# A hybrid encoder layer: softmax denominators moved behind the value products, key decay moved to ScalarE, sums of w_out moved into transfers

## The chip, the cores and the metric

The kernel runs on one core of a Trainium2 chip. TensorE (PE) multiplies, VectorE (DVE), ScalarE (ACT) and GpSimd (POOL) work element by element, SyncE (SP) issues transfers. Each engine works through its own instructions in order and waits for the others by semaphores. The metric is the device time of one execution in microseconds (us); the median of three runs of the kernel before is 1170.45 us (1169.81 to 1171.85).

## The reference, cut to what matters

One layer over 1024 tokens of width 1024: a combined input projection, two groups of mixer heads, an output projection, a layer norm, a SwiGLU with a second gated input, another layer norm. All arithmetic is float32. The change lies in the mixers:

```python
u = jnp.einsum('bsd,de->bse', h, w_in[i])
rq, rk, rv, rg, aq, ak, av = jnp.split(u, split_points, axis=-1)
y_ret = _bidirectional_retention(rq, rk, rv, lg_f, lg_b, ret_gn_gain[i], rg)   # 8 heads of 64
y_att = _windowed_gqa(aq, ak, av, attn_sink[i])                                # 8 q heads, 2 kv heads
mix = jnp.einsum('bse,ed->bsd', jnp.concatenate([y_ret, y_att], axis=-1), w_out[i])
...
# windowed attention: blocks of 128 queries, 384 keys around them, ALiBi slope per head, a sink logit per head
scores = jnp.where(valid, scores + alibi, NEG_INF)
m = jnp.maximum(jnp.max(scores, axis=-1, keepdims=True), sink_l)
e = jnp.exp(scores - m)
denom = jnp.sum(e, axis=-1, keepdims=True) + jnp.exp(sink_l - m)
probs = e / denom
out = jnp.einsum('bnhgqs,bnshd->bnqhgd', probs, vb)
...
# retention, chunks of 128: keys times a decay per row and head, for either direction
kv = jnp.einsum('bhnsd,bhnse->bhnde', k * k_decay[None, :, None, :, None], v)
```

## The kernel before, in words

A float32 product is made of three products of a high part and a low part (`mm3`); the high part is copied by ACT, the low part is subtracted by DVE (`split`). The mixer stage lies at about 50 to 342 us. Its main stream on PE is the rest of the input projection, 128 columns at a time (`mtile`), cut into steps of three matmuls of 128x512, called ticks below. Between these steps, in an order written out by hand (`run` with its lists), PE does the small products of the mixers: `F` in such a list stands for an equal share of the ticks, `sco`, `trn`, `val` for the attention's scores, transposes and value products of a query block, `K`, `kv`, `Q`, `Y`, `E`, `M` for parts of the retention. PE's order is fixed by this list; the orders of ACT, DVE, POOL and SP in this stage are a scheduler's. There are four pairs of heads: for pair 0 the attention and then the retention, for pairs 1 to 3 both woven together, 48 ticks each.

Attention: for each of 8 query blocks (4 to a half, two heads g each) `scores(n)` makes the products, DVE adds the bias, scales and takes the row maximum from PSUM (L550) and negates it (L552), ACT takes the exponential and its row sum (L554), with one more column that POOL copied from the sink logits (L545). Three ticks later DVE takes the reciprocal of the sum (L558) and ACT scales the probabilities by it (L560). `turn(n)` transposes them on PE (L572) and ACT brings them to SBUF (L574); `values(n)` multiplies (L584), and after the fourth block of a half ACT evicts the output (L587).

Retention: `keys(q)` transposes the keys (L408) and DVE multiplies them by the decays from PSUM (L411). `evict` squares the output twice on ACT (L488, L489) and copies it on DVE (L490); `norm` sums the squares on PE (L498), DVE scales the row (L500), and then a chain of small steps brings the normaliser to all partitions: SP spreads the row (L505, tile sn), POOL takes the power (L508), SP stores (L511) and fetches (L515, tile kv or rb), DVE multiplies y by it (L519).

Beside that, weights for later stages are prepared ("presplit"): SP loads a block, DVE sums pieces where the later product wants sums (L638 for w_out, L663 for the gate), `put` splits the piece on ACT and DVE (L602, L603) and SP stores it to DRAM at once (L604). For w_out's blocks 2 and 3 and the small ones all puts of a block share one buffer, so each waits for the store before it.

After the mixers the output projection starts (products at L802 to L804); its left operands are splits of the mixers' outputs y and of sums of them (L71, L72, L869, L871).

Of the kernel before, what the change touches and what calls it, by code (L numbers as in the profile page):

```python
# [12 lines left out]
ALU = mybir.AluOpType  # L13
# [17 lines left out]
LAG = 3  # L31
# [11 lines left out]
def layer(tc, xT, xn, w_first, w_mt, w_rv, w_out, w_pg, w_pe, pT, w_gu, w_dn,  # L43
# [175 lines left out]
    nlg = cp.tile([P, 16], F32, name="nlg")  # L219
    dve.tensor_tensor(nlg, rr[:, 0:16], t_[:, 0:16], ALU.mult)  # L220
# [10 lines left out]
    def slope(i, g):  # L231
        return 2.0 ** -(i + 4 * g + 1)
# [11 lines left out]
    def ev_aq(b, qs, h, i):  # L244
        sl = slice(h * HF, (h + 1) * HF)
        for g in range(2):
            sc_ = 0.125 / slope(i, g)
# [33 lines left out]
    later, side, ticks = [], [], [0]  # L281

    def take(k):
        for _ in range(min(k, len(queue))):
            queue.pop(0)()
            ticks[0] += 1
            for what in (later, side):
# [105 lines left out]
    class Retention:  # L393
# [8 lines left out]
        def keys(self, q):  # L402

            i = self.i
            tb = bank("t", (P, 4, P))
            for j in range(4):
                n = 4 * q + j
                pe.transpose(tb[:, j, :], self.rk[:, n * P:(n + 1) * P], ident)  # L408
            kdec = self.kdec[q] = bt([P, 2, 4, P], ("qq", "pt")[q])
            for d in range(2):  # L410
                dve.tensor_tensor(  # L411
                    kdec[:, d].rearrange("p n (h e) -> p n h e", h=2),
                    tb.rearrange("p n (h e) -> p n h e", h=2),
                    kd[:, d, 2 * i:2 * i + 2].unsqueeze(1).unsqueeze(3).to_broadcast([P, 4, 2, 64]),
                    ALU.mult)
# [69 lines left out]
        def evict(self, hh):  # L485
# [4 lines left out]
            dve.tensor_copy(self.half(hh), of)  # L490
# [35 lines left out]
    class Attention:  # L526


        def __init__(self, i, y):
            self.i, self.y, self.qs = i, y, pairs[i][2]  # L530
            self.st, self.sc, self.pt, self.o, self.ready = {}, {}, {}, {}, set()

        def scores(self, n):
# [9 lines left out]
            sc = self.sc[n] = [bt([P, NKT + 4], "sc", NSC) for _ in range(2)]  # L543
            for g in range(2):
                pool.tensor_copy(sc[g][:, nk:nk + 1], skb[:, 2 * i + g:2 * i + g + 1])  # L545
            for g in range(2):
# [4 lines left out]
                                         skb[:, 2 * i + g:2 * i + g + 1], ALU.add, ALU.max, st_[:, 0, j, g:g + 1])  # L551
            dve.tensor_scalar(st_[:, 1, j, :], st_[:, 0, j, :], -1.0, None, ALU.mult)  # L552
            for g in range(2):
                act.activation(sc[g][:, :nk + 1], sc[g][:, :nk + 1], AF.Exp, bias=st_[:, 1, j, g:g + 1],  # L554
                               accum_out=st_[:, 2, j, g:g + 1])

            def scaled():
                behind(dve.reciprocal(st_[:, 3, j, :], st_[:, 2, j, :]))  # L558
                for g in range(2):
                    behind(act.activation(sc[g][:, :nk], sc[g][:, :nk], AF.Copy, scale=st_[:, 3, j, g:g + 1]))  # L560
                self.ready.add(n)

            later.append((ticks[0] + LAG, scaled))

        def turn(self, n):
            assert n in self.ready
            lo, hi = span(n)
            self.pt[n] = []
            for g in range(2):
# [5 lines left out]
                self.pt[n].append(p_)  # L575

        def values(self, n):
# [8 lines left out]
            if j == 3:  # L586
                act.activation(self.half(hh), self.o[hh], AF.Copy)  # L587
# [6 lines left out]
    rnd = dr.tile([8, P, 8], F32, name="rnd")  # L594
    pgd = dr.tile([7, 4, P, 2, HF], F32, name="pgd")
# [5 lines left out]
    def put(x, o, dst):  # L601
        behind(act.activation(o[:, 0, :], x, AF.Copy))  # L602
        behind(dve.tensor_tensor(o[:, 1, :], x, o[:, 0, :].bitcast(F32), ALU.subtract))  # L603
        sp.dma_start(dst, o.bitcast(F32))  # L604
# [19 lines left out]
    def presplit_out(kt, ops, start, gap, raws=()):  # L624
# [10 lines left out]
        def step(p, k, k2, i):  # L635
            x = hold[k]
            if k2 is not None:
                behind(dve.tensor_tensor(x, x, hold[k2], ALU.add))  # L638
# [4 lines left out]
            [(ticks[0] + start + 5 + gap * i, lambda i=i, a=a: step(*a, i)) for i, a in enumerate(todo)]  # L643
# [95 lines left out]
    with tc.manual_schedule(engines={mybir.EngineType.PE}):  # L739
# [45 lines left out]
        run([*V, F, F, F], 16)  # L785

# [1108 lines left out]
def const_table():  # L1895
# [10 lines left out]
    c[:, C_BASE:C_BASE + NKT] = np.where(d <= P, -d, np.float32(-1e33))  # L1906
# [68 lines left out]
```

## Time and profile before

| what | value |
|---|---|
| median of three runs | 1170.45 us (1169.81 to 1171.85) |
| the profiled execution | span 1166.3 us; nothing beside the span is given for it, the median is 4.2 us above |
| PE busy | 1154.7 us, 99% of the span |
| DVE / ACT / POOL busy | 903.6 / 576.1 / 124.4 us |
| chain that ended last | PE 94%, DVE 3%, DMA 1%, ACT 1% |
| granted PE clock | 0.998 |

A line such as "L411 DVE TENSOR_TENSOR ... x8 | 5.5, 684 | 0.1" reads: line 411 of the kernel, the engine, the operation, how often, then busy time in us, mean duration of one in ns, and idle time of the engine just before. A row of the chain gives start, duration and what. Matmuls overlap, so the distance between their starts, and not the duration of one, is what a further one costs.

### The profile page before, as it was taken

The numbers are of one execution on the slowest core, as the hardware profiler recorded it, in microseconds if no ns is written. First come the engines' busy times: TensorE is split into PE (matmuls) and PEld (weight loads), VectorE is DVE, ScalarE is ACT, GpSimd is POOL, SyncE is SP. The second block draws the span as 40 slices with busy tenths as digits, with TensorE's granted clock in tenths as the row PEclk, the third lists the DMA queues.
The fourth block names the chain that finished last, engine by engine and source line by source line (L and its number), as shares of the span: only waits on it lengthen the run. The fifth ranks groups of instructions, "written<-read, shape, count | busy, mean of one in ns | idle before, by whom it ended". The sixth has DMA issues, their size and how long they took to land.

```text
span 1166.3 us, 17917 instructions
## 1 busy us (share of the span) xinstructions
PE 1154.7 (99%) x6330; PEld 971.3 (83%) x6330; DVE 903.6 (77%) x1746; ACT 576.1 (49%) x1169; POOL 124.4 (11%) x182
## 2 busy tenths in 40 slices
PE   9999999999999999999999999999999999999997
PEld 7888888888887888888888888888888888888885
DVE  5666697877859788948999988889888976864678
ACT  5566358676756265214445433444344445552462
POOL 2001021202010020000000000000000020234243
PEclk9999999999999999999999999999999999999999
DMA  6345676646356955665232232232223289989978
GB/s 253 103 150 205 254 236 215 209 154 218 132 192 231 359 181 197 250 218 197 100 116 92 101 120 103 85 137 99 100 72 136 94 253 350 351 220 225 254 157 234
DMA packets 84377, 214.39 MB, mean 184 GB/s; under 512 B 12224, under 2 KB 17472, under 8 KB 84288
## 3 DMA queue, kind: packets, MB, share of 16 engines
q1 hardware_dynamic: 75504, 195.94, 47.6%
q0 software_dynamic: 8784, 17.31, 8.4%
q8 instruction: 50, 0.82, 0.3%
q14 instruction: 39, 0.32, 0.1%
HBM read 141.32 MB, written 62.16 MB: 174 GB/s over the span
## 4 chain that ended last, share of the span: by engine, by line
PE 94%; DVE 3%; DMA 1%; ACT 1%; issue 1%; POOL 0%; SPq 0%; DVEq 0%; POOLq 0%; ACTq 0%
PE bmm L802 8%; PE bmm L803 8%; PE bmm L804 8%; PE bt L802 6%; PE bt L803 6%; PE bt L804 6%; PE bmm L77 5%; PE bmm L78 5%; PE bmm L79 5%; PE bs L804 4%; PE bs L803 4%; PE bs L802 4%; PE bo L804 4%; PE bo L803 4%; PE bo L802 4%; PE bt L572 2%
## 5 line engine op out<-in xcount | busy, mean ns | idle before, releaser
L77 PE MATMUL bmm<-H,w 128*128 128x512 f32 x240 | 97.0, 404 | 0.0
L78 PE MATMUL bmm<-H,w 128*128 128x512 f32 x240 | 94.1, 392 | 0.0
L79 PE MATMUL bmm<-H,w 128*128 128x512 f32 x240 | 93.9, 391 | 0.0
L1561 POOL DMA_DIRECT2D h0b<-in_w_dn x24 | 21.6, 902 | 538.4 <-DVE ev L1367 503.6
L1387 ACT ACTIVATE ev<-ev 128x512 f32<-128x512 f32 x42 | 26.5, 631 | 103.7 <-DVE ev L1416 90.5
L77 PEld LDWEIGHTS bmm<-H,w 128*128 128x128 f32 x240 | 45.1, 188 | 11.0 <-issue 1.4
L79 PEld LDWEIGHTS bmm<-H,w 128*128 128x128 f32 x240 | 45.0, 188 | 10.2
L78 PEld LDWEIGHTS bmm<-H,w 128*128 128x128 f32 x240 | 45.1, 188 | 8.3 <-DVE H L72 0.4
L554 ACT ACTIVATE sc<-sc,st 128x385 f32<-128x385 f32 (+1 forms) x64 | 37.3, 586 | 27.1 <-DVE st L552 27.0
L550 DVE CUSTOM_DVE_ANT_0 sc<-cst,bs,skb 128x384 f32<-128x384 f32 (+1 forms) x64 | 34.9, 575 | 7.7 <-PE bs L549 7.4
L1416 DVE TENSOR_TENSOR ev<-ev,bt 128x512 f32<-128x512 f32 x44 | 30.1, 684 | 12.6 <-PE bt L804 12.5
L1367 DVE TENSOR_TENSOR ev<-ev,bs 128x256 f32<-128x256 f32 x63 | 25.6, 418 | 15.5 <-PE bs L804 14.7
L545 POOL COPY sc<-skb 128x1 f32<-128x1 f32 x64 | 17.4, 280 | 189.2 <-PE bt L572 163.2
L1389 DVE TENSOR_TENSOR ev<-ev 128x512 f32<-128x512 f32 x42 | 29.0, 691 | 10.6 <-ACT ev L1387 9.1
L802 PE MATMUL bmm<-H,u 128*128 128x512 f32 x92 | 36.1, 392 | 0.0
L803 PE MATMUL bmm<-H,u 128*128 128x512 f32 x92 | 36.0, 392 | 0.0
L804 PE MATMUL bmm<-H,u 128*128 128x512 f32 x92 | 35.8, 389 | 0.0
L71 ACT ACTIVATE H<-ln 128x512 fp32r<-128x512 f32 (+1 forms) x34 | 23.0, 679 | 24.1 <-DVE ln L1051 7.2
L560 ACT ACTIVATE sc<-sc,st 128x384 f32<-128x384 f32 (+1 forms) x64 | 34.2, 583 | 0.9 <-DVE st L558 0.9
L72 DVE TENSOR_TENSOR w<-raw,w 128x512 fp32r<-128x512 f32 x34 | 23.1, 688 | 13.9 <-ACT w L71 13.9
L574 ACT ACTIVATE ptr<-bt 128x384 f32<-128x384 f32 (+1 forms) x64 | 26.6, 458 | 12.9 <-PE bt L572 12.7
L802 PE MATMUL bmm<-H,w 128*128 128x512 f32 x84 | 32.9, 392 | 0.0
(802 smaller groups left out, 3903.0 us busy)
## 6 DMA issues: line engine op xcount, KB each, us to landing
ad<-ev SPq DMA_DIRECT2D x33, 512.0 KB, 2.6
pgd<-pro SPq DMA_DIRECT2D x28, 512.0 KB, 2.9
raw<-in_w_gu SPq DMA_DIRECT2D x22, 512.0 KB, 3.7
ln<-in_w_gu SPq DMA_DIRECT2D x22, 512.0 KB, 3.8
raw<-ad SPq DMA_DIRECT2D x40, 256.0 KB, 5.8
ln<-ad SPq DMA_DIRECT2D x37, 256.0 KB, 6.3
H<-in_w_dn SPq DMA_DIRECT2D x33, 256.0 KB, 7.1
wod<-aq SPq DMA_DIRECT2D x15, 512.0 KB, 2.7
```

Source lines behind the costliest of these rows:

```text
L77: pe.matmul(o, lh, rh, start=start, stop=False)
L78: pe.matmul(o, lh, rl, start=False, stop=False)
L79: recent[0] = pe.matmul(o, ll, rh, start=False, stop=stop).ins.name
L550: dve.tensor_tensor_reduce(sc[g][:, :nk], cst[:, tc0:tc0 + nk], b[:, :nk], slope(i, g), skb[:, 2 * i + g:2 * i + g + 1], ALU.add, ALU.max, ...
L554: act.activation(sc[g][:, :nk + 1], sc[g][:, :nk + 1], AF.Exp, bias=st_[:, 1, j, g:g + 1], accum_out=st_[:, 2, j, g:g + 1])
L560: behind(act.activation(sc[g][:, :nk], sc[g][:, :nk], AF.Copy, scale=st_[:, 3, j, g:g + 1]))
L574: act.activation(p_[:, :hi - lo, :], tb[:, :hi - lo, :], AF.Copy)
L802: pe.matmul(o, lh, rh, start=start, stop=False, skip_group_check=True)
L803: pe.matmul(o, lh, rl, start=False, stop=False, skip_group_check=True)
L804: pe.matmul(o, ll, rh, start=False, stop=stop, skip_group_check=True)
L1389: dve.tensor_tensor(c[:, 1, :], c[:, 0, :], c[:, 1, :], ALU.mult)
L1416: dve.tensor_tensor(get(name), ev[left][:, m, :], right, ALU.add)
```

## The change

The exponentials go into the value products undivided; the division follows them. For that the scores are kept with the opposite sign: the scale of the attention's queries and the distance table change sign, the row maximum becomes a minimum that is itself the bias of the exponential (which takes scale -1), so the negation (L552) goes, and the sink column on POOL goes too. When the fourth block of a half has its scores, `sums` (two ticks later) adds exp(sink - m) for all four blocks and takes one reciprocal. `spread` follows block 2's or 6's transposes: PE turns the 128x8 reciprocals to 8x128, ACT copies them to SBUF, SP stores them to DRAM one tick later and, from the fifth tick on, fetches them twice, each spread over 64 partitions, into the place of the output in y. After the fourth value product DVE multiplies PSUM by y there, in place of ACT's copy.

The keys' decay is four ACT copies with a scale for each half in place of two DVE products; retention's copy of its output goes from DVE to ACT. The pieces of w_out are summed by transfers that POOL issues, reading w_out again and adding into the loaded tile; the order of the seven puts changes with it. `put` no longer issues its store at once: the store comes with the next put into the same buffer, or 2.5 ticks later.

PE gets eight rows more and keeps its order otherwise. The new row stands behind the transposes of block 2 of pair 3 (bt is the PSUM tile of the transposes, sc the exponentials, st the reciprocals):

```order
L586 MATMUL bt_3280<-cst,sc_3156 128x128 x3
L586 MATMUL bt_3286<-cst,sc_3157 128x128 x3
L566 MATMUL bt_3286<-cst,st_3016 8x128
L545 MATMUL bs_3298<-k_410,aq_2893 128x384
L546 MATMUL bs_3298<-kz_412,aq_2893 128x384
```

Before, the first two rows (then at L572) were followed by the scores at once.

DVE at the start of pair 2, before (kd are the keys' decays, w a weight split, aq the next queries):

```order
L500 TENSOR_SCALAR kv_2288<-bo_2201 2x512
L72 TENSOR_TENSOR w_2335<-raw_2333,w_2335 128x512
L519 SCALAR_TENSOR_TENSOR y_1604<-y_1604,gn,kv_2116 128x512
L411 TENSOR_TENSOR qq_2330<-bt_2325,kd 128x512
L251 SCALAR_TENSOR_TENSOR aq_2248<-bmm_2254,aq_2248 64x512
L411 TENSOR_TENSOR qq_2330<-bt_2325,kd 128x512
L72 TENSOR_TENSOR w_2338<-raw_2333,w_2338 128x512
L251 SCALAR_TENSOR_TENSOR aq_2249<-bmm_2254,aq_2249 64x512
L411 TENSOR_TENSOR pt_2360<-bt_2355,kd 128x512 x2
```

and after the change:

```order
L499 TENSOR_SCALAR kv_2239<-bo_2147 2x512
L72 TENSOR_TENSOR w_2290<-raw_2288,w_2290 128x512
L518 SCALAR_TENSOR_TENSOR y_1581<-y_1581,gn,kv_2067 128x512
L251 SCALAR_TENSOR_TENSOR aq_2193<-bmm_2200,aq_2193 64x512
L251 SCALAR_TENSOR_TENSOR aq_2194<-bmm_2200,aq_2194 64x512
L72 TENSOR_TENSOR w_2293<-raw_2288,w_2293 128x512
```

The four products with kd are gone from this place; the multiplication by the fetched row (L518, before L519) keeps its place.

SP at the end of pair 3, before (ped are stores of the last puts, sn and rnd and rb the last norm chain, w the first load of the next stage):

```order
L604 DMA ped<-aq_3046 128x1024
L505 DMA sn_3719<-kv_3717 64x1x8 x2
L511 DMA rnd<-sn_3719 128x8
L604 DMA ped<-aq_3046 128x1024
L515 DMA rb_3720<-rnd 64x512 x2
```

and after the change (adn holds the reciprocals):

```order
L623 DMA ped<-aq_2974 128x1024
L571 DMA adn<-rows_3600 8x128
L843 DMA w_3738<-wod 128x1024
L575 DMA y_2277<-adn 64x4x128
L623 DMA ped<-aq_2974 128x1024
L575 DMA y_2277<-adn 64x4x128
L504 DMA sn_3621<-kv_3619 64x1x8 x2
L510 DMA rnd<-sn_3621 128x8
L514 DMA rb_3622<-rnd 64x512 x2
```

The last store and the three transfers of the reciprocals now stand ahead of the norm chain's first transfer (sn).

The diff, without the constants' sign and the tile that goes:

```diff
@@ decay_k
             behind(act.activation(e[:, d, :], cst[:, C_BASE + P:C_BASE + 2 * P], AF.Exp,
-                                  scale=nlg[:, 8 * d + 2 * i + h:8 * d + 2 * i + h + 1]))
+                                  scale=lg[:, 8 * d + 2 * i + h:8 * d + 2 * i + h + 1]))
@@ Retention.keys
             for d in range(2):
-                dve.tensor_tensor(
-                    kdec[:, d].rearrange("p n (h e) -> p n h e", h=2),
-                    tb.rearrange("p n (h e) -> p n h e", h=2),
-                    kd[:, d, 2 * i:2 * i + 2].unsqueeze(1).unsqueeze(3).to_broadcast([P, 4, 2, 64]),
-                    ALU.mult)
+                for h in range(2):
+                    e = slice(64 * h, 64 * h + 64)
+                    act.activation(kdec[:, d, :, e], tb[:, :, e], AF.Copy, scale=kd[:, d, 2 * i + h:2 * i + h + 1])
@@ Retention.evict
-            dve.tensor_copy(self.half(hh), of)
+            act.activation(self.half(hh), of, AF.Copy)
@@ Attention.scores
-            for g in range(2):
-                pool.tensor_copy(sc[g][:, nk:nk + 1], skb[:, 2 * i + g:2 * i + g + 1])
...
                 dve.tensor_tensor_reduce(sc[g][:, :nk], cst[:, tc0:tc0 + nk], b[:, :nk], slope(i, g),
-                                         skb[:, 2 * i + g:2 * i + g + 1], ALU.add, ALU.max, st_[:, 0, j, g:g + 1])
-            dve.tensor_scalar(st_[:, 1, j, :], st_[:, 0, j, :], -1.0, None, ALU.mult)
+                                         nskb[:, 2 * i + g:2 * i + g + 1], ALU.add, ALU.min, st_[:, 0, j, g:g + 1])
             for g in range(2):
-                act.activation(sc[g][:, :nk + 1], sc[g][:, :nk + 1], AF.Exp, bias=st_[:, 1, j, g:g + 1],
+                act.activation(sc[g][:, :nk], sc[g][:, :nk], AF.Exp, bias=st_[:, 0, j, g:g + 1], scale=-1.0,
                                accum_out=st_[:, 2, j, g:g + 1])
-
-            def scaled():
-                behind(dve.reciprocal(st_[:, 3, j, :], st_[:, 2, j, :]))
+            if j < 3:
+                return
+
+            def sums():
                 for g in range(2):
-                    behind(act.activation(sc[g][:, :nk], sc[g][:, :nk], AF.Copy, scale=st_[:, 3, j, g:g + 1]))
-                self.ready.add(n)
+                    behind(act.activation(st_[:, 1, :, g], st_[:, 0, :, g], AF.Exp, bias=skb[:, 2 * i + g:2 * i + g + 1]))
+                behind(dve.tensor_tensor(st_[:, 2], st_[:, 2], st_[:, 1], ALU.add))
+                behind(dve.reciprocal(st_[:, 3], st_[:, 2]))
...
+        def spread(self, hh, b):
+
+            rows, home = bt([8, P], "rows", 1), adn[2 * self.i + hh]
+            pe.transpose(b, self.st[hh][:, 3].rearrange("p j g -> p (j g)"), ident)
+            act.activation(rows, b, AF.Copy)
+            r = self.y[:, hh * HF:(hh + 1) * HF]
+
+            def store():
+                sp.dma_start(home, rows)
+
+            def fetch():
+                for g in range(2):
+                    sp.dma_start(r[64 * g:64 * g + 64].rearrange("p (j q) -> p j q", j=4),
+                                 home.rearrange("(j g) q -> g j q", g=2)[g].partition_broadcast(64))
+
+            later.extend((ticks[0] + at, f) for at, f in zip(LAGA[1:], (store, fetch)))
@@ Attention.turn, Attention.values
+                if g and n % 4 == 2:
+                    self.spread(n // 4, tb[0:8, 3, :])
...
-                act.activation(self.half(hh), self.o[hh], AF.Copy)
+                dve.tensor_tensor(self.half(hh), self.o[hh], self.half(hh), ALU.mult)
@@ put
+        if id(o) in unsaved:
+            unsaved.pop(id(o))()
         behind(act.activation(o[:, 0, :], x, AF.Copy))
         behind(dve.tensor_tensor(o[:, 1, :], x, o[:, 0, :].bitcast(F32), ALU.subtract))
-        sp.dma_start(dst, o.bitcast(F32))
+        unsaved[id(o)] = save = lambda: sp.dma_start(dst, o.bitcast(F32))
...
+        saves.append((ticks[0] + 2.5, due))
@@ presplit_out
-        def step(p, k, k2, i):
-            x = hold[k]
-            if k2 is not None:
-                behind(dve.tensor_tensor(x, x, hold[k2], ALU.add))
-            put(x, ops[i % len(ops)], wod[p - 1, kt])
-
-        todo = ((1, 0, None), (2, 2, None), (3, 3, None), (5, 0, 1), (7, 1, 3), (6, 0, 3), (4, 0, 2))
+        def add(k, k2):
+            behind(pool.dma_start(hold[k], w_out[kt + 4 * (k2 // 2)][:, (k2 % 2) * HF:(k2 % 2 + 1) * HF], accum_op=ALU.add))
+
+        def step(i, p, k, *sums):
+            for x in sums:
+                add(*x)
+            put(hold[k], ops[i % len(ops)], wod[p - 1, kt])
+
+        todo = ((1, 0), (2, 2, (0, 1)), (5, 0), (3, 3, (0, 3), (1, 3)), (6, 0), (7, 1, (0, 2)), (4, 0))
```

More of the change, by code (lines that the diff above doesn't have):

```diff
@@ L30 @@
 NSC = 4
-LAG = 3
+LAGA = (2, 1, 5)
 LAGS = (3, 6, 9, 12, 15)
@@ L218, in layer @@
     dve.scalar_tensor_tensor(lg, rr, -1.0, t_, ALU.mult, ALU.mult)
-    nlg = cp.tile([P, 16], F32, name="nlg")
-    dve.tensor_tensor(nlg, rr[:, 0:16], t_[:, 0:16], ALU.mult)
+    nskb = cp.tile([P, 8], F32, name="nskb")
+    dve.tensor_scalar(nskb, skb, -1.0, None, ALU.mult)
     kd = cp.tile([P, 2, 8], F32, name="kd")
@@ L246, in ev_aq @@
         for g in range(2):
-            sc_ = 0.125 / slope(i, g)
+            sc_ = -0.125 / slope(i, g)
             a = slice(64 * g, 64 * g + 64)
@@ L278, in layer @@
     queue = []
-    later, side, ticks = [], [], [0]
+    later, side, saves, ticks = [], [], [], [0]
+    unsaved = {}
     def take(k):
@@ L286, in take @@
             ticks[0] += 1
-            for what in (later, side):
+            for what in (later, side, saves):
                 for x in [x for x in what if x[0] <= ticks[0]]:
@@ L530, in __init__ @@
             self.i, self.y, self.qs = i, y, pairs[i][2]
-            self.st, self.sc, self.pt, self.o, self.ready = {}, {}, {}, {}, set()
+            self.st, self.sc, self.pt, self.o = {}, {}, {}, {}
         def scores(self, n):
@@ L542, in scores @@
             qc = slice(n * P, (n + 1) * P)
-            sc = self.sc[n] = [bt([P, NKT + 4], "sc", NSC) for _ in range(2)]
-            for g in range(2):
-                pool.tensor_copy(sc[g][:, nk:nk + 1], skb[:, 2 * i + g:2 * i + g + 1])
+            sc = self.sc[n] = [bt([P, NKT], "sc", NSC) for _ in range(2)]
             for g in range(2):
@@ L594, in layer @@
     rnd = dr.tile([8, P, 8], F32, name="rnd")
+    adn = dr.tile([8, 8, P], F32, name="adn")
     pgd = dr.tile([7, 4, P, 2, HF], F32, name="pgd")
@@ L601, in put, with due @@
     def put(x, o, dst):
+        if id(o) in unsaved:
+            unsaved.pop(id(o))()
         behind(act.activation(o[:, 0, :], x, AF.Copy))
         behind(dve.tensor_tensor(o[:, 1, :], x, o[:, 0, :].bitcast(F32), ALU.subtract))
-        sp.dma_start(dst, o.bitcast(F32))
+        unsaved[id(o)] = save = lambda: sp.dma_start(dst, o.bitcast(F32))
+        def due():
+            if unsaved.get(id(o)) is save:
+                unsaved.pop(id(o))()
+        saves.append((ticks[0] + 2.5, due))
     def presplit_small(n, o, start, raw=None, other=None):
@@ L633, in load @@
                 hold.extend([r[:, :HF], r[:, HF:]])
-        def step(p, k, k2, i):
-            x = hold[k]
-            if k2 is not None:
-                behind(dve.tensor_tensor(x, x, hold[k2], ALU.add))
-            put(x, ops[i % len(ops)], wod[p - 1, kt])
-        todo = ((1, 0, None), (2, 2, None), (3, 3, None), (5, 0, 1), (7, 1, 3), (6, 0, 3), (4, 0, 2))
+        def add(k, k2):
[5 more added lines that the diff above has]
+        todo = ((1, 0), (2, 2, (0, 1)), (5, 0), (3, 3, (0, 3), (1, 3)), (6, 0), (7, 1, (0, 2)), (4, 0))
         return [(ticks[0] + start, load)] + \
-            [(ticks[0] + start + 5 + gap * i, lambda i=i, a=a: step(*a, i)) for i, a in enumerate(todo)]
+            [(ticks[0] + start + 5 + gap * i, lambda i=i, a=a: step(i, *a)) for i, a in enumerate(todo)]
     def presplit_gate():
@@ L785, in layer @@
         run([*V, F, F, F], 16)
+        while unsaved:
+            unsaved.popitem()[1]()
     bp.close()
@@ L1905, in const_table @@
     d = np.abs(np.arange(NKT, dtype=np.float32)[None, :] - P - s)
-    c[:, C_BASE:C_BASE + NKT] = np.where(d <= P, -d, np.float32(-1e33))
+    c[:, C_BASE:C_BASE + NKT] = np.where(d <= P, d, np.float32(1e33))
     c[:, C_KF] = P - 1 - s[:, 0]
```

3 lines of the change are left out of this document (1 added, 2 removed).

## The prediction

> **What bounds the kernel now.** I read the page first, then the busy time by stages, then PE's waits, and last the chain around each wait.
>
> ```profile
> span 1166.3 us, 17917 instructions
> PE 1154.7 (99%) x6330; PEld 971.3 (83%) x6330; DVE 903.6 (77%) x1746; ACT 576.1 (49%) x1169; POOL 124.4 (11%) x182
> ```
>
> PE is idle for 11.6 us of the whole span. By stages (columns: length, then busy time of PE, PEld, DVE, ACT and POOL with counts, then clock, DMA share and GB/s):
>
> ```profile
> 120.00:342.00 222.00, 221.36 (x1728) 185.16 (x1727) 174.21 (x406) 145.05 (x340) 33.09 (x63) 1.00 0.58 201
> 342.00:366.00 24.00, 22.91 (x101) 18.53 (x100) 18.38 (x31) 13.73 (x26) 1.64 (x1) 1.00 0.65 234
> 366.00:1120.00 754.00, 754.00 (x3730) 640.07 (x3729) 604.20 (x1089) 325.57 (x619) 59.14 (x61) 1.00 0.55 178
> 1120.00:1167.00 47.00, 37.74 (x167) 30.94 (x165) 37.59 (x78) 20.10 (x39) 15.85 (x20) 0.94 0.68 173
> ```
>
> The woven pairs of mixers (120 to 342) leave PE idle for 0.6 us, the step into the output projection (342 to 366) for 1.1 us, and nothing is lost from there to 1120; the last 47 us, with 9 us idle, hold none of the changed work. DVE is busy 78% of the mixers, ACT 65%: neither is the bound, and their work counts only where it makes PE wait. PE's own list of waits:
>
> ```profile
> ...
> PE bt L802 <- ACT h0b L971: 1.1, 1, 1.1
> PE bs L548 <- DVE pt L461: 0.5, 1, 0.5
> PE bt L572 <- ACT sc L560: 0.2, 1, 0.2
> ```
>
> Left out is one at the kernel's start. These three, 1.8 us together, are all that a better order on the other engines can win. The 0.5 us at 233 us comes out of this chain (start, duration, what):
>
> ```profile
> 218.07 3.73 DMA kv<-rnd
> 221.91 0.75 DVE y L519
> 222.66 0.60 DVE qq L411
> ...
> 226.03 1.29 DVE pt L411 x2
> ...
> 232.60 0.70 DVE pt L461
> 233.34 0.44 PE bs L548
> ```
>
> DVE has stood still for the fetched row, then works through the keys' decays, and comes late to the scores' eviction L461. The 1.1 us ends another chain:
>
> ```profile
> 338.69 3.75 DMA sn<-kv
> ...
> 342.60 1.65 POOL sn L508
> ...
> 346.22 3.95 DMA rb<-rnd
> ...
> 351.02 1.09 DVE H L72 x2
> ...
> 364.33 0.49 ACT h0b L971
> ...
> 364.87 0.50 PE bt L802
> ```
>
> The last normaliser lands at 350.2 (346.22 + 3.95); DVE multiplies by it (L519) and from there prepares operands without a pause, and the eviction h0b that PE waits for stands on ACT behind an operand that needs them. If the row comes x us sooner or later, this wait moves by x, down to nothing.
>
> **The change, part by part.** Prices of single operations (mean in ns after the comma):
>
> ```profile
> L560 ACT ACTIVATE sc<-sc,st 128x384 f32<-128x384 f32 (+1 forms) x64 | 34.2, 583 | 0.9 <-DVE st L558 0.9
> L411 DVE TENSOR_TENSOR qq<-bt,kd 128x512 f32<-128x512 f32 x8 | 5.5, 684 | 0.1
> L434 ACT ACTIVATE kv<-bt 128x256 f32<-128x256 f32 x4 | 1.5, 378 | 0.7 <-DVE kv L436 0.7
> L490 DVE COPY y<-bo 128x512 f32<-128x512 f32 x8 | 5.5, 690 | 5.9 <-ACT pt L489 4.9 <-ACT kv L489 1.0
> L587 ACT ACTIVATE y<-bo 128x512 f32<-128x512 f32 x8 | 4.8, 595 | 4.9 <-PE bo L584 4.9
> L638 DVE TENSOR_TENSOR y<-y,raw 128x512 f32<-128x512 f32 x3 | 2.0, 681 | 0.0
> L603 DVE TENSOR_TENSOR aq<-rk,aq 128x512 fp32r<-128x512 f32 x6 | 4.1, 690 | 1.4 <-ACT aq L602 1.4
> L572 PE MATMUL bt<-cst,sc 128*128 128x128 f32 x176 | 24.8, 274 | 0.2 <-ACT sc L560 0.2
> ```
>
> and from the chain, a run of six transposes, a run of value products and one projection matmul:
>
> ```profile
> 91.77 1.46 PE bo L584 x24
> ...
> 206.00 0.65 PE bt L572 x6
> ...
> 214.01 0.23 PE bmm L77
> ```
>
> *PE.* Eight transposes more. Six of the existing kind take 0.65 us, 0.11 each: 8 x 0.11 = 0.9 us, all on the path. Had each to stand alone, its whole duration would show, 8 x 0.274 = 2.2; it follows transposes into the same bank, so I take 0.9.
>
> *Off the path.* ACT loses 64 scalings (34.2 us) and eight evictions (4.8), and gains 32 decays at about 0.38 (12.1, by the row of 256 columns), eight copies at 0.6 (4.8) and 24 small ones: some 17 us less. DVE loses 16 products of 0.684 (10.9), eight copies (5.5), sixteen sums of 0.68 (10.9) and the small negations and reciprocals, and gains eight multiplications of about 0.7: more than 20 us less. POOL loses the sink columns and gains 16 issues of transfers. None of it is worth anything by itself, PE hides it all. What it does is to take the two waits inside the mixers away: the four decays leave DVE's chain at 222 to 227 (2.7 us against a wait of 0.5), and L560, for which PE waited 0.2, is gone, with the reciprocal ahead of it. **-0.7 us.** The decays on ACT need at most 8 x 0.38 = 3 us per pair before the products `kv`, six ticks later. If that cover failed, DVE's gain would return as an ACT wait; I take 0 there.
>
> A tick is about 1.25 us in the pairs: these two outputs stand one pair, 48 ticks, apart.
>
> ```profile
> 194.84 1.90 PE bo L481 x32
> ...
> 254.65 1.90 PE bo L481 x32
> ```
>
> *Sums by transfers.* Three puts in each of four blocks, twelve in all, now wait on ACT for a sum to land. The transfer can leave once the put before the last has read the tile, so it has two gaps of at least 3.1 ticks less that put's work: 7.7 - 1.3 = 6.4 us (a put is 0.6 on ACT, as L587, and 0.69 on DVE, L603). The kernel issues such adding transfers elsewhere (first row: POOL's own time, ns; second: us from issue to landing):
>
> ```profile
> L1561 POOL DMA_DIRECT2D h0b<-in_w_dn x24: 866/876/1194, 944.0 to 1119.1; - x24
> ...
> DMA to landing us min/median/max: 4.5/6.7/8.7
> ```
>
> ACT is early by 1.9 to late by 2.3 us, 0.3 late at the median. Behind it in line stand exponentials and evictions of transposes; the nine matmuls between two transposes cover 9 x 0.23 = 2.1 us of that, so PE sees 0 to 0.2 each, at most 2.4 us in all. I take 0, since the median's 0.3 lies inside the cover.
>
> *The multiplication.* DVE now waits for a fetched row where ACT waited for nothing. From the fifth tick after block 2's transposes there are about two ticks (2.5), an output (1.9) and the value products (1.4) to the multiplication, 5.8 us, for two issues and a fetch. A like fetch (kv, rb) takes
>
> ```profile
> DMA to landing us min/median/max: 2.7/3.5/5.2
> ```
>
> so with 1 us of issue it is early by 2 or late by 0.4. Behind the waiting DVE stand the scores' evictions, on which PE's next bank hangs. I take 0, and 0.4 for each of eight as the upper end (3 us).
>
> *Stores later, and the last norm chain.* SP's new order puts the last store and two fetches ahead of the row's first transfer. SP before, at that place:
>
> ```profile
> 337.57 0.33 SPq L604 DMA_DIRECT2D ped<-aq  x1
> 338.16 1.44 SPq L505 DMA_DIRECT2D sn<-kv  x2
> ```
>
> and the list of transfers (KB each, median us from issue to landing):
>
> ```profile
> ped<-aq SPq DMA_DIRECT2D x3, 512.0 KB, 3.0
> ```
>
> The last put waits for the third store to land (3.0 us), then takes 1.3 us on ACT and DVE: 337.6 + 3.0 + 1.3 = 341.9, and with a fetch's issue 342.4 against 338.2, 4.2 us late, if the puts run as before. They have four sums of 0.68 fewer in their chain, 2.7 us; that leaves 1.5 us. DVE's order gives something back: two of the operand splits (1.2 us, the row of 351.02) now stand ahead of L519, so DVE fills the wait. Net +0.3 us on the wait at 364. Its ends: -1.1 (the wait goes) and 4.2 - 1.2 = +3.0.
>
> **The sum:** 0.9 - 0.7 + 0 + 0 + 0.3 = +0.5 us. Against the profiled span 1166.3 that is 1166.8; the 4.2 us between span and median stay, and **1170.9 us** is the forecast, no change by the bound of 0.2% (2.3 us) that a measurement here can tell.
>
> **The rivals.**
>
> *The wait at 364 closes.* The puts come early enough that the norm chain starts at 338 as before, and DVE's new order removes the 1.1 us. For it: puts lose the sums. Against: the third store still has to land before the last put. 0.9 - 0.7 - 1.1 = -0.9: 1169.5 us.
>
> *The last store holds the norm chain.* If the last store leaves SP after about 341, more than two splits' time late, each further us goes to PE. For it: SP's order, and the single buffer. At the full 4.2 late: 0.9 - 0.7 + 3.0 = +3.2, 1173.6 us, slower.
>
> *DVE stands at the multiplication.* The second fetch of pair 1 is ordered behind two loads and a store; a stretch of 1 us at each half of pairs 1 to 3, beyond the slack, gives 6 x 0.7 = 4.2 more: 1175.1 us. Against: DVE has been relieved of more than that just before each place.
>
> *The adding transfers are starved.* DVE's work holds up what POOL issues, and the sums land late. If landing went to 10.5 us, ACT would be held 4.1, PE 2.0 at twelve places: 24 us, 1194 us. The rows speak against it: with DVE busy 80% of the stretch 366 to 1120, POOL's own time for such an issue went from 866 to at most 1194 ns. [...]
>
> **How the numbers follow.** Forecast 0.52, the wait closes 0.22, the norm chain held 0.12, the multiplication 0.10, starved transfers 0.04. Forecast and closing wait both lie within 2.3 us of 1170.45, as do the milder halves of the next two: same 0.72. Slower 0.22 is the rest of the last three and a tail of the forecast with its dearer transposes. Faster 0.06: the three waits are 1.8 us in all and the transposes cost half of that, so only the spread of the runs (2 us) can bring it. The range: 1169.5 less 0.6, the spread of the runs shown below their median, gives 1168.9; above, the held norm chain, 1173.6, and a little of the multiplication: 1174.0.
>
> **What would show it.** PE's waits without L461 and without the scaling; the transposes of st at 0.11 us from start to start; no new wait of PE in 50 to 342 over 0.5 us; SP's sn of the last chain at 338 to 341, and the wait before the eviction h0b at 0 to 1.5 us; sums landing in 4.5 to 7 us. It is wrong if PE has waits of the scores' banks on DVE (the multiplication), of transposes on ACT (the sums), or loses over 2 us at the step into the output projection.

## The result, and the profile after

The changed kernel takes 1184.32 us (median of four runs, 1181.28 to 1185.41) against 1170.14 us (median of four): ratio 1.0111, interval 1.0098 to 1.0125. By this ratio it is 13 us slower (the medians lie 14.2 apart), where the forecast was 1170.9 and the range ended at 1174.0. Differences in microseconds between kernels are worked out from the ratios below, too. The profiled execution took 1183.48 us with this head of its page:

```profile
span 1181.7 us, 17767 instructions
PE 1159.3 (98%) x6338; PEld 973.3 (82%) x6338; DVE 879.6 (74%) x1666; ACT 563.5 (48%) x1161; POOL 122.4 (10%) x134
```

VectorE lost 24 us of work and ScalarE 13, near what was worked out beforehand (20 and 17), and PE gained its eight transposes. But PE is idle for 22.4 us where it was idle for 11.6. Here the span lies 1.8 us below the execution's own time, and in the later runs of the kernel before about 2.1 us. The profile of before lies 4.2 us below its kernel's median, so it had caught an execution some 2 us faster than the median, and spans compared overstate the loss by as much.

Busy times by stages of the changed kernel (columns as in the prediction):

```profile
120.00:342.00 222.00, 213.80 (x1628) 177.63 (x1626) 149.43 (x333) 135.79 (x333) 28.47 (x30) 0.99 0.66 211
366.00:1120.00 754.00, 752.73 (x3720) 638.30 (x3719) 609.05 (x1097) 328.48 (x626) 53.15 (x55) 1.00 0.56 179
```

From 120 to 342 PE is idle for 8.2 us instead of 0.6; behind 366 1.3 us are new, all at the start of that stretch. PE's own waits say what for:

```profile
PE bt L566 <- ACT ptr L588: 7.0, 8, 1.8
PE bt L586 <- ACT ptr L588: 2.2, 1, 2.2
PE bs L545 <- DVE pt L460: 2.0, 3, 1.0
...
PE bt L832 <- ACT h L71: 0.6, 1, 0.6
PE bt L832 <- DMA w<-wod: 0.4, 1, 0.4
PE bt L832 <- DMA u<-wod: 0.4, 1, 0.4
```

The first row is new: L566 is the transpose of the reciprocals' tile `st`, and all eight wait, for ScalarE's eviction `ptr`. One of them in the order of time (start, duration, engine, line, idle time ahead and what ended it):

```profile
81.44 0.87 PE L586 MATMUL bt<-cst,sc 128*128 128x128 f32 x6
82.02 0.87 ACT L588 ACTIVATE ptr<-bt 128x384 f32<-128x384 f32 x2 [2.28 <-PE bt L586]
82.95 0.08 PEld L566 LDWEIGHTS bt<-cst,st 128*8 128x8 f32 x1 [0.87 <-ACT ptr L588]
82.95 0.27 PE L566 MATMUL bt<-cst,st 128*8 128x128 f32 x1 [0.63 <-ACT ptr L588]
82.95 0.19 PEld L545 LDWEIGHTS bs<-k,aq 128*128 128x128 f32 x1
82.98 0.42 PE L545 MATMUL bs<-k,aq 128*128 128x384 f32 x1
```

The six transposes of the exponentials end, ScalarE copies their two banks out, and only behind the second copy does PE write its eight rows into the fourth quarter of the second bank, which the copy does not read. The next product starts 0.03 us behind the transpose, so here the wait is all of its price. With each PE instruction matched to its counterpart in the trace of before, the eight places put PE back by 9.2 us, from the start of the last transpose ahead to the start of the next product (the expectation of e1 below counts 8.6). The rest of the 15.4 us by which the spans differ is one stall of 2.2 us at 212 with some 3 us at half clock behind it (4 us), the three waits for the scores' eviction L460, and late operand loads at 368, less the wait at 364, which is gone.

### The profile page after: what moved, and what is told of

It reads as the page before. It is cut to its first block, busy times and chain, and to the rows that moved or that the text cites. A ratio compares the mean times of both kernels' runs of the same rounds, so it can differ in the third digit from the quotient of the medians.

```text
span 1181.7 us, 17767 instructions
## 1 busy us (share of the span) xinstructions
PE 1159.3 (98%) x6338; PEld 973.3 (82%) x6338; DVE 879.6 (74%) x1666; ACT 563.5 (48%) x1161; POOL 122.4 (10%) x134
## 4 chain that ended last, share of the span: by engine, by line
PE 86%; DMA 5%; DVE 4%; ACT 2%; issue 1%; POOL 0%; SPq 0%; DVEq 0%; ACTq 0%; POOLq 0%
PE bmm L832 8%; PE bmm L833 8%; PE bmm L834 8%; PE bt L832 6%; PE bt L833 6%; PE bt L834 6%; PE bs L834 4%; PE bs L833 4%; PE bs L832 4%; PE bmm L77 4%; PE bmm L78 4%; PE bmm L79 4%; PE bo L834 4%; PE bo L833 4%; PE bo L832 4%; DMA pgd<-pro 2%
## 5 line engine op out<-in xcount | busy, mean ns | idle before, releaser
L77 PE MATMUL bmm<-H,w 128*128 128x512 f32 x240 | 97.3, 406 | 0.0
L78 PE MATMUL bmm<-H,w 128*128 128x512 f32 x240 | 94.3, 393 | 0.0
L79 PE MATMUL bmm<-H,w 128*128 128x512 f32 x240 | 94.2, 393 | 0.0
L550 ACT ACTIVATE sc<-sc,st 128x384 f32<-128x384 f32 (+1 forms) x64 | 37.2, 586 | 14.4 <-DVE st L547 14.2
L547 DVE CUSTOM_DVE_ANT_0 sc<-cst,bs,nskb 128x384 f32<-128x384 f32 (+1 forms) x64 | 34.8, 575 | 12.2 <-PE bs L546 12.1
L1419 DVE TENSOR_TENSOR ev<-ev 128x512 f32<-128x512 f32 x42 | 29.0, 691 | 10.5 <-ACT ev L1417 9.0
L832 PE MATMUL bmm<-H,w 128*128 128x512 f32 x84 | 33.0, 392 | 0.0
L833 PE MATMUL bmm<-H,w 128*128 128x512 f32 x84 | 32.9, 392 | 0.0
L834 PE MATMUL bmm<-H,w 128*128 128x512 f32 x84 | 32.7, 389 | 0.0
```

Source lines behind the costliest of these rows:

```text
L77: pe.matmul(o, lh, rh, start=start, stop=False)
L78: pe.matmul(o, lh, rl, start=False, stop=False)
L79: recent[0] = pe.matmul(o, ll, rh, start=False, stop=stop).ins.name
L547: dve.tensor_tensor_reduce(sc[g][:, :nk], cst[:, tc0:tc0 + nk], b[:, :nk], slope(i, g), nskb[:, 2 * i + g:2 * i + g + 1], ALU.add, ALU.min ...
L550: act.activation(sc[g][:, :nk], sc[g][:, :nk], AF.Exp, bias=st_[:, 0, j, g:g + 1], scale=-1.0, accum_out=st_[:, 2, j, g:g + 1])
L832: pe.matmul(o, lh, rh, start=start, stop=False, skip_group_check=True)
```

## The experiments

Every ratio below is against runs of the kernel before on the same chip.

**The bank, and the late stores.** Four kernels start from the changed one. e1 moves one instruction in `turn`, and nothing else:

```diff
+                if g and n % 4 == 2:
+                    pe.transpose(tb[0:8, 3, :], self.st[n // 4][:, 3]..., ident)
                 p_ = bt([P, 3, P], "ptr", 4)
                 act.activation(p_[:, :hi - lo, :], tb[:, :hi - lo, :], AF.Copy)
```

> The changed kernel with one instruction moved: each of the eight transposes of st is issued ahead of ScalarE's eviction of the bank it writes, not behind it. Theory A (the bank): in the changed kernel PE stands 0.63 to 1.8 us at each of the eight transposes, 7.0 us in all and 8.6 us of shift against the kernel before, because the transpose writes a bank that ScalarE is still reading. Seven of the eight reciprocals are there 2 us or more earlier, so with the order turned round the wait should go, all but 0.5 us at the second: about 1176 us, and no wait of PE on the eviction ptr at L566's place. Theory B (the other engines are late by then anyway, and the eight stalls only give them time): the waits come back as waits of the scores' banks on VectorE or of the transposes on ScalarE, and the time stays at or above 1181.

e2 issues each store behind its put again:

```diff
-        unsaved[id(o)] = save = lambda: sp.dma_start(dst, o.bitcast(F32))
...
-        saves.append((ticks[0] + 2.5, due))
+        sp.dma_start(dst, o.bitcast(F32))
```

> The changed kernel with each store issued right behind its put, as before the change; all else as changed. Theory A (late stores): the four other stalls of the changed kernel in the mixers (1.19 us at 177, 2.40 at 211 with 1.5 us of half clock behind it, 0.63 at 273, 0.66 at 335) and the late operand loads at 368 (1.8 us) come from stores that leave SP 2.5 ticks later, so that the next put stands on ScalarE until they land. They go: 1184.3 - 6 = about 1178 us, with the eight stalls of st left. Rival (the fetched reciprocals and the adding transfers fill the queues): the stalls stay, 1183 to 1185.

e3 has both edits:

> Both edits, the transpose of st ahead of the eviction and the stores at once. If the two causes are separate and are all there is, the sum of what each gives: 1170 to 1171 us. If the stalls at the transposes hid lateness of VectorE or ScalarE, part comes back: 1173 to 1177.

e4 gives the sums back to VectorE:

```diff
-            behind(pool.dma_start(hold[k], w_out[...][...], accum_op=ALU.add))
+            behind(dve.tensor_tensor(hold[k], hold[k], hold[k2], ALU.add))
```

> The changed kernel with the sixteen sums of w_out done by VectorE again (in the new order of the pieces), no adding transfers. The prediction put the adding transfers at 0 (their lateness of 0.3 us lies inside PE's cover): 1184 +- 1 us. If VectorE's 10.9 us more matter at the places where PE waits for its eviction of the scores (178, 273, 335): 1185 to 1187. If the adding transfers are starved or slow the stores, below 1181.

Measured: e1 1181.25 us, 1.0085 (1.0069 to 1.0100); e2 1182.19, 1.0094 (1.0078 to 1.0111); e3 1176.97, 1.0045 (1.0031 to 1.0060); e4 1181.05, 1.0081 (1.0069 to 1.0093). For e1 the rival held, with 3 us given back and not 8; e2 gave 2 and not 6; e3 came out at the end of its second range; e4, put at nothing, gave 3. The two longest of PE's waits in e1:

```profile
PE bs L545 <- DVE pt L460: 2.6, 2, 1.8
PE bt L585 <- ACT ptr L589: 2.3, 2, 1.2
```

The eight waits at the transpose are gone, and waits stand elsewhere. That fits the rival, by which the other engines were late too and the stalls had given them time. Edits undone one by one in a kernel with several faults therefore did not price the parts.

**Each part alone.** So the four parts were put one by one into the kernel before; the edits are the parts of the diff.

> The kernel before with one part of the change alone: the sixteen sums of w_out made by adding transfers that GpSimd issues (with the new order of the pieces). In the changed kernel, sums on VectorE gave back 3.3 us. Theory A: that is the transfers' own price (a put on ScalarE waits 5 to 6.5 us for a sum to land, in a chain of seven puts that has no reserve): 1173 to 1174. Theory B: the sums cost only where the other parts have already eaten the reserve; alone they cost nothing, as the prediction had it: 1170.5 to 1171.5.

> The kernel before with one part alone: the keys' decay by ScalarE (32 products of 128x256) and the copy of the retention output on ScalarE. The prediction: the wait of PE for VectorE's L461 at 233 (0.5 us) goes, ScalarE's extra 3 us per pair is covered: 1170 to 1170.5. Rival (ScalarE comes late to the exponentials or to kv): 1172 or more.

> The kernel before with one part alone: each store issued 2.5 ticks (3 us) after its put, or at the next put into the same buffer. Undoing this in the changed kernel gave 2.1 us alone and 4.3 us with the eight stalls gone. If the next put then stands on ScalarE until the later store has landed, and the operand loads after the mixers go out later: 1173 to 1175. If a kernel without the other parts has the reserve: 1171.

> The kernel before with one part alone: scores negated, denominators turned by PE, stored, fetched and applied behind the value products. Theory A (bank): eight stalls of PE at the transpose of st, 0.8 us each at least, and the transposes' own 0.9: 1170.9 + 7.5 = 1178 to 1179, with no further waits on VectorE's L460. Theory A with the queue: SP also stands some 6 us at the fetch of half 1 of pair 0 until the small store of the rows has landed, and the gate's loads behind it come late; then stalls at 140 to 180 and a time of 1180 to 1183. If the other parts are needed to make it slow: 1172 to 1175.

Measured: sums 1169.27, 0.9987 (0.9978 to 0.9996); keys 1168.10, 0.9977 (0.9965 to 0.9989); later stores 1172.65, 1.0015 (1.0006 to 1.0024); denominators 1179.81, 1.0080 (1.0065 to 1.0095). In microseconds: -1.5, -2.7, +1.8, +9.4, together 7 of the 13; the other 6 arise only between the parts. Sums, forecast at 0, and keys, forecast at -0.7, both came out a little better than forecast; later stores and denominators each came out between the two ranges of their expectation. PE's longest wait of the denominators alone:

```profile
PE bt L567 <- ACT ptr L589: 9.3, 8, 3.1
```

Then the denominators alone with the transpose ahead of the eviction, the same edit as e1:

> The kernel before with the denominators' part alone, and in it the transpose of st ahead of ScalarE's eviction of its bank. With the eviction ahead this part cost 9.0 us (1179.8), with 9.3 us of waits of PE at the eight transposes. Theory A (the bank is the whole price of this part): the eight waits go and what is left is the transposes' own 0.9 us: 1171 to 1173. Rival (the store and the fetches of the reciprocals hold SP's queue, and the waits return elsewhere, as with the same edit in the whole change, where only 3.1 of 8 us came back): 1175 to 1177.

1169.43, 0.9987 (0.9978 to 0.9995). One instruction moved ahead of the eviction takes 1.0080 to 0.9987, 11 us of 1170 (by the trace of the part alone the eight places put PE back by 11.5): here the wait for the eviction is the whole price of this part. In c1's trace each of the eight transposes moves PE on by 0.11 us, 0.9 in all, just what the prediction took; the run is still below the 1171 to 1173 expected, and what makes up for the 0.9 was not traced. PE's waits there, but for the one at the kernel's start:

```profile
PE bt L821 <- DMA u<-wod: 1.3, 2, 0.9
PE bt L586 <- ACT rows L567: 0.7, 1, 0.7
PE bt L821 <- DMA w<-wod: 0.4, 1, 0.4
PE bt L428 <- PE bt L428: 0.2, 1, 0.2
```

No row is left of the eight waits; what comes instead is one wait of 0.7 us, for ScalarE to take the reciprocals' rows out of the bank, and late operand loads (L821).

**What makes the parts dear together.** Three parts that each gain alone (c1, keys, sums) are e3, +0.45%. Pairs of them:

> The kernel before with the two parts that gained alone: keys' decay and copy on ScalarE (1168.1 alone) and the sums by adding transfers (1169.3 alone). If the gains add: 1170.8 - 2.7 - 1.5 = 1166.6. If both take away the same waits of PE (1.8 us in all): 1168. If together they eat the reserve of ScalarE's puts, as in the whole change: above 1170.

> The kernel before with the denominators' part (transpose of st ahead of the eviction; 1169.4 alone) and the keys' part (1168.1 alone); sums on VectorE, stores at once. With the sums as transfers too this is 1177.0, though each of the three parts alone is below the kernel before. Theory A (the sums are what breaks it: a put stands on ScalarE until a sum has landed, exponentials and reciprocals behind it are late, the small store of the rows falls behind a 512 KB load): 1167 to 1169, SP stands under 1.5 us at the fetch at 109. Theory B (ScalarE is short of time once the keys' decays, the rows and the small exponentials are all on it): 1172 to 1177.

> The same denominators' part with the sums by adding transfers, keys' decay on VectorE. Theory A: 1174 to 1177, SP stands 5 us or more at the fetch of half 1 of pair 0. Theory B: 1168 to 1171.

Keys and sums: 1168.45, 0.9981 (0.9972 to 0.9990), no better than the keys alone; these two are the fastest kernels of the study. Denominators and keys: 1169.63, 0.9986 (0.9977 to 0.9996). Denominators and sums: 1179.57, 1.0076 (1.0063 to 1.0089), above the range of either theory. It is the sums with the denominators. SP's issues of c1, without the sums (start, time on SP):

```profile
107.69 0.29 SPq L571 DMA_DIRECT2D adn<-rows  x1
108.96 1.25 SPq L575 DMA_DIRECT2D y<-adn  x2
111.18 0.34 SPq L623 DMA_DIRECT2D wod<-aq  x1
```

and of d2, with them:

```profile
107.73 0.46 SPq L111 DMA_DIRECT2D raw<-in_w_mt  x1
108.28 0.88 SPq L571 DMA_DIRECT2D adn<-rows  x1
114.98 0.58 SPq L575 DMA_DIRECT2D y<-adn  x1
115.66 0.61 SPq L623 DMA_DIRECT2D wod<-aq  x1
```

From the issue of the 4 KB store (`adn<-rows`) to the fetch that needs it pass 1.3 us in the one and 6.7 us in the other. SP stands at that fetch, and the next store of w_out behind it leaves 4.5 us later. ScalarE in d2 (idle time ahead in brackets):

```profile
104.09 0.63 ACT L621 ACTIVATE aq<-states 128x512 fp32r<-128x512 f32 x1 [4.15 <-DMA states<-in_w_out]
...
110.93 0.63 ACT L621 ACTIVATE aq<-states 128x512 fp32r<-128x512 f32 x1 [2.84 <-DMA states<-in_w_out]
...
121.41 0.63 ACT L621 ACTIVATE aq<-states 128x512 fp32r<-128x512 f32 x1 [7.14 <-DMA wod<-aq]
```

First it stands for two sums, then 7.1 us for that store. After it come the gate's puts and pair 0's retention. Against the trace of before PE is put back by 4.4 us between 140 and 175 (c1: nothing), and by 2.9 at 362, where it waits for operand loads (c1: 1.0).

Three edits of e3 tried SP's stand: the store and the fetches on GpSimd's queue (c2), the store on ScalarE's queue (d3), and the store ahead of the load in SP's queue by an added order between the two (f1).

```diff
-                sp.dma_start(home, rows)
+                pool.dma_start(home, rows)          # c2, and the fetches too
+                act.dma_start(home, rows)           # d3
+                rowed[0] = sp.dma_start(home, rows).ins.name    # f1; the load is ordered behind it
```

> The changed kernel with both edits (transpose of st ahead, stores at once; 1177.0), and with the store of the rows and the fetches of the reciprocals issued by GpSimd instead of SP. Theory A (SP stands): in that kernel SP stood 5.9 us at the fetch of half 1 of pair 0, at 110 to 116, until the small store behind a 512 KB load had landed; the gate's loads behind it left 6 us late and PE lost 4.9 us at 146 to 170. That goes: about 1172, and the gate's loads leave at 111 to 114. Theory B (other reasons: ScalarE carries the keys' decays, copies and puts late in pair 0): 1176 to 1178.

> The changed kernel with transpose ahead and stores at once (1177.0), and the small store of the rows issued by ScalarE, right behind its eviction of them, so that it does not stand behind the 512 KB load in SP's queue. Theory A (SP's stand of 5.9 us at the fetch, and with it the late store of the w_out piece, the next put 6 us late on ScalarE and the gate's loads, is what costs 5 us of PE between 146 and 170): the store lands in 1 to 2 us, SP goes on at 111, 1171 to 1173. If the late sum on ScalarE at 100 to 105 is enough by itself: 1175 to 1177.

> The changed kernel with transpose ahead and stores at once (1177.0), and one pair of rows of SP's queue exchanged: the small store of the rows of pair 0, half 1, goes ahead of the 512 KB load of weights that the planner had put ahead of it. Theory (the load ahead is the link: the store lands 5.9 us late, SP stands at the fetch with the w_out store and the gate's loads behind it): the store lands in 1 to 2 us as in the kernel with VectorE's sums, the next w_out store leaves at 111 to 112 and not 116, PE's stalls at 146 to 170 (4.9 us) go: 1171 to 1173. If ScalarE's stand for the sum at 98 to 104 costs the rest by itself: 1175 to 1177.

c2: 1178.29, 1.0064 (1.0050 to 1.0077). d3: 1174.64, 1.0035 (1.0022 to 1.0047). f1: 1176.62, 1.0052 (1.0040 to 1.0064). None is the cure. In c2 GpSimd stands at the fetch instead, 6.9 us behind the store's issue, with the last sum of the block behind it:

```profile
ACT aq L622 <- DMA states<-in_w_out: 15.9, 3, 9.5
```

and in d3, by the chain of work, the store still needs

```profile
108.25 5.46 DMA adn<-rows
```

In f1 SP stands 4.1 us at the fetch though the store left ahead of the load. So the theory of the order in the queue falls: it is not the load ahead of the store. (Two stores of w_out still stand ahead of it there; in d3, on ScalarE's queue, they don't.) What d2, e3 and f1 have in common is how full the DMA engines are just then: the share from 108 to 110 is 0.99, 0.89 and 0.90 (not shown for c2 and d3). In the rows the columns are as before; the last but one is the DMA share. The kernel before:

```profile
108.00:110.00 2.00, 2.00 (x10) 1.65 (x10) 1.90 (x4) 0.88 (x3) 0.00 (x0) 1.00 0.00 0
110.00:112.00 2.00, 2.00 (x13) 1.65 (x12) 1.14 (x3) 1.51 (x5) 1.15 (x4) 1.00 0.36 147
```

and d2:

```profile
108.00:110.00 2.00, 2.00 (x11) 1.63 (x10) 1.38 (x2) 0.09 (x1) 0.00 (x0) 1.00 0.99 125
110.00:112.00 2.00, 2.00 (x13) 1.66 (x12) 0.41 (x1) 1.07 (x3) 0.00 (x0) 1.00 1.06 266
```

Two adding transfers, a load of 512 KB and two stores of 512 KB are issued between 105.5 and 108 in d2, when ScalarE has come free of the first sum and makes two puts at once. But full DMA engines are not the loss by themselves. The sums alone (b1), which gain, fill them as much:

```profile
108.00:110.00 2.00, 2.00 (x10) 1.69 (x9) 1.73 (x3) 1.04 (x3) 0.00 (x0) 1.00 1.06 358
110.00:112.00 2.00, 2.00 (x12) 1.65 (x12) 0.10 (x1) 1.18 (x3) 1.19 (x4) 1.00 1.01 416
```

ScalarE stands for sums in b1 too (once for 5.4 us, until 117.3), and yet PE is not put back at all up to 176 us. What b1 lacks is the small store with SP standing behind it. The last run therefore took only the sums of that one block of w_out back to VectorE (e3 otherwise):

```diff
         def add(k, k2):
+            if kt == 1:
+                behind(dve.tensor_tensor(hold[k], hold[k], hold[k2], ALU.add))
+            else:
                 behind(pool.dma_start(...))
```

> The changed kernel with transpose ahead and stores at once (1177.0), and the four sums of the one block of w_out that falls into pair 0's attention (76 to 122 us) made by VectorE; the other three blocks keep their adding transfers. The exchange of store and load alone (1176.6) left SP standing 4.1 us: the DMA engines are busy 0.9 to 1.06 of the time from 108 to 114 in the kernels that lose there (two adding transfers, a 512 KB load and a 512 KB store together), against 0.0 to 0.44 in the kernel before and 0.01 to 0.66 with VectorE's sums. Theory A (this block's sums make the burst, and hold ScalarE from 98 to 104): SP stands under 1.5 us at the fetch, DMA share below 0.7 there, PE's shift at 146 to 170 under 1 us: 1170 to 1172. If the sums of the later blocks (230 to 330 us) cost as much: 1174 to 1176.

1171.43 us, 1.0000 (0.9990 to 1.0009). Its SP:

```profile
107.29 0.29 SPq L570 DMA_DIRECT2D adn<-rows  x1
108.55 0.59 SPq L574 DMA_DIRECT2D y<-adn  x1
110.30 0.34 SPq L624 DMA_DIRECT2D wod<-aq  x1
```

The fetch follows the store in 1.3 us, SP waits 1.0 of them, and PE is put back by 0.9 us at 164. The DMA share from 108 to 110 is 0.02. Not all of the expectation is met: from 112 to 114 the share is 0.80, above the 0.7 named, after the store had long landed. Of the 5.3 us that e3 lost, these four sums, beside the denominators, made all that can be told from the kernel before; what is left against denominators and keys alone (1.0000 to 0.9986) lies where the intervals touch. Which of their two effects weighs more there, ScalarE's stand or the full DMA engines, no run separates; b1 shows that both together cost nothing without the denominators.

**The later stores without the rest.** f2 is f1 with the stores later again.

> The same with the stores 2.5 ticks later as in the change: what the later stores cost once the other two causes are gone. 4.3 us were found in the change with the transposes ahead, 1.8 us in the kernel before. If those 4.3 us had the stand of SP in them: f1 plus 2, 1173 to 1175; if they are the stores' own: f1 plus 4, 1175 to 1177.

1179.97, 1.0087 (1.0071 to 1.0103): 1.0087 - 1.0052 is 4 us, much as in e1 against e3 (4.7), and more than the 1.8 us of b3. Since f1 had not removed SP's stand, this does not say what the stores cost without it. How they act shows in ScalarE's waits of the changed kernel between 60 and 345 us:

```profile
ACT pro L621 <- DMA pgd<-pro: 12.9, 7, 4.9
ACT aq L621 <- DMA wod<-aq: 12.8, 5, 6.0
```

Puts stand there until the store of the same buffer has landed. With stores at once and nothing else changed (e2) the first row falls to 6.0 us and the second stays at 12.8; in c2, where the fetches no longer stand in SP's queue, the second is 5.7, so about half of it goes with SP's stand.

## Why the prediction was wrong

**The step that failed first** is "it follows transposes into the same bank, so I take 0.9". That was taken as a reason for cheapness and is the reason for the price: between those transposes and this one stands ScalarE's eviction of the bank. The upper end of 2.2 us priced an instruction and no wait; the wait came to 9.2 us in the changed kernel's trace and to 11 in the part alone, most of the miss of 13. The 0.9 itself was right as the price of eight transposes that don't wait (c1). The code showed the wait, since `spread` was called behind the eviction, on the same tile; at its shortest, 0.63 us, it is most of two evictions, one of each bank, which take 0.87 us together. No rival held it. The row named as the sign of late sums, PE waiting for ScalarE at transposes, did come, but from here: e4, with the sums on VectorE, has the same eight waits (8.0 us).

In the trace of the changed kernel the eight rows lie in a quarter of the bank that the eviction doesn't read (it reads 128x384 of 128x512), in partitions that it does read, and all eight transposes waited, 7.0 us in all. What the kernel allots as a bank is one tile of 128x512, so no run separates a wait for the tile from one for the memory that it lies in.

**The sums at 0** held alone (-1.5 us) and failed together with the denominators (+8.9, d2). Their landing was forecast well (4.5 to 7 us; by medians 5.0 to 5.7 came). The wrong number was the time that they have: "two gaps of at least 3.1 ticks less that put's work", 6.4 us. A planned gap is not a real one. In the changed kernel the puts on ScalarE at 96.8 and 98.0 are 1.1 us apart, the sum leaves at 98.8, and the next put wants it at 101.2, 2.4 us later; it stands 4.15. Nor do three puts of a block wait for a sum, but four, the fourth with a gap more. That "the median's 0.3 lies inside the cover" looked at what stands behind on ScalarE, and not at the puts, stores and loads that are pushed together and at the small store that has to pass through them.

**Stores later** were priced only at the last norm chain (+0.3), and for the stores by themselves that place was nearly right: in b3 the wait at 364 falls from 1.1 us to 0.6, with one of 0.4 beside it, and PE is put back by 0.1 there. Not priced was every other place where a put follows a store into the same buffer: 1.8 us alone, 2 to 4.7 us beside the other parts. The stall at 212 is such a place: ScalarE had just stood 4.9 us for a store (`pgd<-pro`), and in e2, with the stores at once, PE has no wait there.

**The late operand loads** were not in the forecast. In SP's queue they stand behind the last norm chain's fetch (rb), before the change and after it. With the denominators this fetch leaves some 2.4 us later against PE: at 349.0 in c1, where PE is 0.9 late by then, and at 345.7 before. With later stores alone it is not late (347.4, PE 1.6). In the changed kernel PE is put back by 1.9 us at 368, where it waits for the loads, less 1.2 for the wait at 364, which closes: +0.7 net, inside the ends given. Both c1 and d1 have such waits for loads, and none of b1, b2, b3 and c3 has. The prediction followed the late chain to VectorE's operands and not to the loads behind it.

**The waits that go (-0.7)** was right in kind: neither the kernel with the keys' part alone nor c1 has the wait for the scores' eviction at 233. It was too small: -2.7 for the keys. The three waits quoted came from an execution some 2 us faster than the median, so the usual one has probably more to win than they showed; that was not traced.

**The multiplication (0)** was nearly right. VectorE does stand for the fetched rows, three times:

```profile
DVE y L603 <- DMA y<-adn: 5.3, 3, 2.9
```

Once PE pays for it, on the path that the prediction had named for its upper end, the scores' eviction behind the waiting VectorE:

```profile
272.04 0.69 DVE L603 TENSOR_TENSOR y<-bo,y 128x512 f32<-128x512 f32 x1 [1.77 <-DMA y<-adn]
272.65 1.28 DVE L460 TENSOR_TENSOR pt<-bs,dt 128x512 f32<-128x512 f32 x2
273.38 0.44 PE L545 MATMUL bs<-k,aq 128*128 128x384 f32 x1 [0.46 <-DVE pt L460]
```

That is 0.5 us of wait and 0.7 us of delay in one of eight places, against an upper end of 0.4 for each.

**The rivals.** The starved transfers did not come: the slowest sum of the changed kernel landed in 6.8 us, not 10.5. GpSimd's own time for such an issue was 0.86 to 1.22 us there; that VectorE's work holds it up was not shown. The slow side came from what no rival named, and from two parts that were each weighed alone.

## What to carry to other kernels

In this kernel a write into a bank that another engine was still emptying waited for the end of the eviction at eight places of eight (7.0 us, and 9.3 with the denominators alone), though it went to a part that the eviction did not read: issue late additions to a bank ahead of its eviction. When work goes from an engine to transfers, look at what else is in flight in the same microseconds, and at the smallest transfer that something waits for. Price parts alone and in pairs: undoing one fault in a kernel with several gave 3 us here, where the same edit gave 11 in the part alone.

## What was not expected of the hardware

**A 4 KB store took 1.3 us or 5.5 to 6.9 us**, from its issue to the fetch that waits for it: 1.3 where the DMA share from 108 to 110 was 0.01 (c1) and 0.02 (f3), and 6.2 in the changed kernel, 6.8 in e3, 5.5 in f1 and 6.7 in d2, where it was 0.87 to 0.99. Neither another engine's queue (6.9 in c2, 5.5 in d3) nor a place ahead of the load (f1) helped much.

**A stall of 2 us cost nearly twice its length.** The changed kernel around the stall at 212 (the clock is the number after POOL's):

```profile
211.70:214.10 2.40, 0.16 (x1) 0.00 (x0) 1.44 (x4) 2.06 (x5) 0.00 (x0) 0.95 0.80 277
214.10:215.30 1.20, 1.20 (x7) 1.20 (x7) 1.20 (x4) 1.20 (x4) 0.00 (x0) 0.50 0.53 106
...
217.40:219.00 1.60, 1.60 (x9) 1.02 (x10) 1.60 (x6) 1.60 (x6) 1.52 (x3) 1.00 0.46 182
```

For 3.3 us PE ran at half clock, 1.6 us more. In the denominators alone (b4), a stall of 3.1 us was followed by full clock, and the half clock came some 1.4 us after PE went on:

```profile
218.90:222.00 3.10, 0.07 (x1) 0.00 (x0) 3.01 (x6) 2.09 (x4) 0.00 (x0) 1.00 0.79 242
222.00:223.00 1.00, 0.96 (x5) 0.82 (x6) 0.52 (x1) 0.65 (x2) 0.00 (x0) 1.00 0.49 193
...
224.00:225.00 1.00, 1.00 (x4) 0.77 (x3) 0.00 (x0) 0.00 (x0) 0.00 (x0) 0.50 0.39 143
```

The stall of 1.8 us at 107 in the changed kernel had no half clock at all (1.00 in each slice from 107 to 113). So it is not the length of the stall alone: 2.2 us had the half clock as soon as PE went on, 3.1 us had it 1.4 us later. What else decides it, and what ended it after 3.3 us, was not shown.
